# Four buffers instead of three and two for the weights between two feed-forward passes of an encoder kernel

## The chip, the cores and the metric

The kernel runs on one core of a Trainium2 chip. The metric is the device time of one execution in microseconds (us); the time before is 1585.03 us, the median of three runs (1584.3 to 1585.76).

## The reference

One encoder layer is applied to a prompt of 512 tokens and to a sample of 1024 tokens, both with 1024 channels, in float32:

```
x    = layer_norm(x)
h    = x @ w_in                               -> conv value | conv gate | rnn x | rnn gate
c    = silu(layer_norm(depthwise_conv31(value * sigmoid(gate))))
rec  = (rg_lru forward + rg_lru backward) * gelu(rnn gate)
x    = layer_norm(ALPHA * x + concat(c, rec) @ w_out)
u    = depthwise_conv3(x @ w_up)              -> val | gate, 2816 channels each
x    = layer_norm(ALPHA * x + (gelu(gate) * val) @ w_down)
```

## The kernel before, in words

The tokens are worked on in blocks of 512: the prompt (blk None), the second half of the sample (blk 1) and its first half (blk 0). Every product is made three times over, from a high and a low part of each operand (hi*hi, hi*lo, lo*hi); a weight therefore lies in SBUF as a pair, hi and lo.

**How a weight is made ready.** `weight` (L480) loads the raw tile (512 KB) into one of three staging buffers ST0 to ST2, and ScalarE (ACT) copies it, rounded, into the hi half of a weight slot. At the first use of a tile VectorE (DVE) or GpSimd (POOL) subtracts to get the lo half, which is then also stored to DRAM (`lo_out_d`, `lo_up_d`, `lo_down_d`); at a later use the lo half comes from there by a second DMA. A weight slot is a name such as W0; a `rot` list hands the names out in turn, and a new tile may enter a slot only when TensorE (PE) has read the old one for the last time.

**The stretch that the change touches** comes twice. In the first hand-over PE goes from the feed-forward pass of the prompt to that of blk 1, in the second from blk 1 to blk 0:

1. `up` tiles of `ffn` (L892): 44 tiles of 24 matmuls, weights in W0, W1, G3 by turns; their results go through three PSUM banks U0 to U2. `down` groups between them use A2, A3.
2. `residual` (L767): the output projection. For each half nh of the 1024 columns four weights kp, each used by 24 matmuls (four token tiles i, six each); slots by the list `WS` (L1014): W0, W1, G3 by turns.
3. `last` (L999): the last group of the down projection (pairs 18 to 21), held back so that PE has work while the layer norm `ln1` of the projection's result runs on DVE, ACT and POOL. It needs four weights of two chunks each: the first two serve nh = 0, the other two nh = 1, 48 matmuls per nh, in groups of twelve (token tile i). Slots: A2, A3 by turns. Between the groups PE transposes the four normalised token tiles (8 matmuls of 128x128 each, L269) for the next pass.
4. The `up` tiles of the next pass, whose input are these transposed tiles (B0 to B3).

**Other users of the slots.** G1 holds, at other times, the input `g` of the sample's token mixer `mixer_s` (L829), and behind it the layer-norm weights `gb` of the finished pass (`gb2a` L1024, `gb2b` L1036), which `ln2` multiplies and adds. A4 is the hi part of the projection's input for its first 512 channels (`split_block` L879, read by kp 0 and 1), then a buffer of `mixer_s` (L831) or of `ffn(0, ...)` (`a5`, L911). `mixer_s(0, ...)` runs beside the up tiles of blk 1: convolutions and scans on DVE, ACT and POOL, and small matmuls on PE (the recurrence gates) that stand between the up tiles.

**What sets the order.** `Sched.emit` (L273) places all operations before the program runs: it walks through a model of the engines and takes, on each, the ready operation of the best priority. What comes out is a fixed order on each engine and on the DMA queue of SP; at run time each engine follows its own order and waits by semaphores. So another slot name changes when an operation counts as ready, and with it the order. All DMAs are issued by SP (L250), one after the other: an issue that waits holds up those behind it.

```
w = weight(ws(), [("out", 4 * nh + kp, ALLC)], prio - 2, lo_eng="any", st=st)      # L767 residual
ws = rot(["W0", "W1", "G3"])                                                        # L898 ffn, up tiles
wdslot = rot(["A2", "A3"])                                                          # L901 ffn, down tiles
```

Of the kernel before, what the change touches and what calls it, by code (L numbers as in the profile page):

```python
# [12 lines left out]
ALU = mybir.AluOpType  # L13
# [5 lines left out]
NPAIR = DFF // 128  # L19
# [353 lines left out]
def body(ctx, tc, xp, xs, w_in, gw, w_out, w_up, w_down, par, gb, out_p, out_s):  # L373
# [3 lines left out]
    S = Sched(tc, sb, ps)  # L377
# [81 lines left out]
    def rot(names):  # L459
        st = {"i": 0}  # L460

        def nxt():
            st["i"] += 1
            return names[(st["i"] - 1) % len(names)]
        return nxt

    def split(hi, lo, src, prio, hi_eng="act", lo_eng="dve"):
        S.copy(hi_eng, hi, src, prio)
        S.tt(lo_eng, lo, src, hi.f32, ALU.subtract, prio)
# [83 lines left out]
    def mtile(w, xq, out, prio, parts=2, cols=slice(0, 512)):  # L553
        for q in range(parts):
            pairs = []
            for k in range(8 // parts * q, 8 // parts * (q + 1)):
                xh, xl = xk(xq, k, cols)
                c = slice(k * 128, (k + 1) * 128)
                pairs += prod3(w[0, c], w[1, c], xh, xl)
            S.mm(out, pairs, q == 0, q == parts - 1, prio)  # L560
# [328 lines left out]
    def tapcol(k):  # L889
        return P[C_FW:C_FW + 6 * NPAIR]._with(lambda a: a.rearrange("p (c k) -> p c k", k=3)[:, :, k])  # L890

    def ffn(blk, x1, y, PR, ev, wprio):  # L892

        va = S.buf("G0", [2, 2, 512])
        fb = [S.buf(n, [2, 2, 512], f32r) for n in (("A0", "A1", "GB") if blk == 0 else ("A0", "A1"))]
        ws = rot(["W0", "W1", "G3"])  # L898
        ub = rot([S.buf(f"U{i}", [512], psum=True) for i in range(3)])
        st = {"db": rot([S.buf(n, [512], psum=True) for n in ("U3", "M2")])}  # L900
        wdslot = rot(["A2", "A3"])  # L901
        first = blk is None
        lo = 1 if blk == 1 else 0
        if blk == 1:
            for b in fb:
                for i in range(2):
                    for h in range(2):
                        z = b[i, h, 0:1]
                        S.op("pool", 100, lambda z=z: nc.gpsimd.memset(z.f32(), 0.0), [], [z], ev)
        if blk == 0:  # L910
            a5 = S.buf("A4", [1024])  # L911
            ex = S.buf("ex", [2, 2])
            S.tt("dve", ut.all, sv[:, 0], tapcol(1), ALU.mult, ev)
            S.tt("dve", ut.all, ut.all, P[C_FB:C_FB + 2 * NPAIR], ALU.add, ev)
            t2 = S.buf("A5", [2 * NPAIR])
            S.tt("dve", t2.all, sv[:, 1], tapcol(2), ALU.mult, ev)
            S.tt("dve", ut.all, ut.all, t2.all, ALU.add, ev)
        def up(p):
            pr = PR + p * 0.01
            for s in range(2):  # L920
                m = s * NPAIR + p
                w = weight(ws(), [("up", m, ALLC)], wprio, lo_eng="any")
                u = ub()
                mtile(w, x1, u.all, pr)
                c = lambda k: col(C_FW + 3 * m + k)
                v = va[p % 2, s]
                acc = lambda a, b: va[p % 2, s, a:b]
                S.act(v, u.all, AF.Identity, c(1), col(C_FB + m), ev)
                S.stt(acc(1, 512), u[0:511], c(0), acc(1, 512), ALU.mult, ALU.add, ev)
                S.stt(acc(0, 511), u[1:512], c(2), acc(0, 511), ALU.mult, ALU.add, ev)  # L930
                if blk == 1:
                    S.copy("dve", sv[m], u[0:2], ev)
                if blk == 0:
                    S.stt(acc(511, 512), sv[m, 0:1], c(2), acc(511, 512), ALU.mult, ALU.add, ev)
                    S.stt(ex[p % 2, s:s + 1], u[511:512], c(0), ut[m:m + 1], ALU.mult, ALU.add, ev)
            S.act(va[p % 2, 1], va[p % 2, 1], AF.Gelu_apprx_tanh, prio=ev)
            if blk == 0:
                S.act(ex[p % 2, 1:2], ex[p % 2, 1:2], AF.Gelu_apprx_tanh, prio=ev)
                S.tt("dve", f5[p:p + 1], ex[p % 2, 0:1], ex[p % 2, 1:2], ALU.mult, ev)
            r = slice(lo, 512)  # L940
            S.tt("pool" if blk is None else "any", va[p % 2, 0, r], va[p % 2, 0, r], va[p % 2, 1, r], ALU.mult, ev)
            f = fb[(p // 2) % len(fb)]
            split(f[p % 2, 0, r], f[p % 2, 1, r], va[p % 2, 0, r], ev, lo_eng="dve")

        def wds(grp):

            chunks = [(nh, p) for nh in range(2) for p in grp]
            wd = {}

            def get(nh, p):  # L950
                if (nh, p) not in wd:
                    c = chunks.index((nh, p)) // 2 * 2
                    cs = chunks[c:c + 2]
                    w = weight(wdslot(), [("down", p_, slice(n_ * 512, (n_ + 1) * 512)) for n_, p_ in cs], wprio + 1,
                               lo_eng="any")
                    for i, ch_ in enumerate(cs):
                        wd[ch_] = (w, i)
                        if blk == 0:
                            n_, p_ = ch_
                            raw = raw_of[id(w)].buf[i * 512:(i + 1) * 512]  # L960
                            o = a5[n_ * 512:(n_ + 1) * 512]
                            if p_ == 0:
                                S.ts("dve", o, raw, f5[p_:p_ + 1], ALU.mult, prio=wprio)
                            else:
                                S.stt(o, raw, f5[p_:p_ + 1], o, ALU.mult, ALU.add, wprio)
                return wd[nh, p]
            return get

        def products(get, nh, i, ps_):
            pairs = []  # L970
            for p in ps_:
                w, ci = get(nh, p)
                wh, wl = w[0, ci * 512:(ci + 1) * 512], w[1, ci * 512:(ci + 1) * 512]
                f = fb[(p // 2) % len(fb)]
                fh, fl = f[p % 2, 0, i * 128:(i + 1) * 128], f[p % 2, 1, i * 128:(i + 1) * 128]
                pairs += [(fh, wh), (fh, wl), (fl, wh)]
            return pairs

        def down(gi, grp, banks=None, pr=None):
            get = wds(grp)  # L980
            pr = pr or PR + (grp[-1] + 0.5) * 0.01
            for nh in range(2):
                for i in range(4):
                    b = banks() if banks else st["db"]()
                    S.mm(b.all, products(get, nh, i, grp), True, True, pr)
                    yv = y[i // 2][i % 2, nh * 512:(nh + 1) * 512]
                    if gi == 0:
                        S.stt(yv, yv, ALPHA, b.all, ALU.mult, ALU.add, ev)
                    else:
                        S.tt("dve", yv, yv, b.all, ALU.add, ev)  # L990

        late = len(GROUPS) - (2 if blk == 0 else 1)
        for gi, grp in enumerate(GROUPS):
            for p in grp:
                up(p)
            if gi < late:
                down(gi, grp)

        def last():  # L999
            nonlocal wdslot  # L1000
            grp = GROUPS[-1]
            if blk != 0:
                banks = rot([S.buf(n, [512], psum=True) for n in ("M2", "C1")])
                down(len(GROUPS) - 1, grp, banks)
                return


            down(late, GROUPS[late], None, PR + 0.2105)
            wdslot = rot(["G2", "A5", "GW", "A6"])
            return wds(grp), grp, products  # L1010
        return last


    WS = ["W0", "W1", "G3"]  # L1014
    xcf1 = mixer_s(1, ("T2", "T3"), 32, 31)
    last_p = ffn(None, x1P, yP, 50.0, 6, 4)
    xc1 = split_block(xcf1, 33)
# [1 line left out]
    UB = ["U3", "M2", "C0", "C1", "U0", "U1", "U2", "U3"]  # L1019
    residual(1, 1, xc1, y1, 40, UB, rot(WS), pe=50.2105)  # L1020
    last_p()
# [9 lines left out]
    y0 = [S.buf("T0", [2, D]), S.buf("T1", [2, D])]  # L1031
    residual(1, 0, xc0, y0, 56, UB, rot(WS), pe=60.2105)
    last_1()
# [89 lines left out]
```

## Time and profile before

| | |
|---|---|
| median of three runs | 1585.03 us |
| the profiled execution | 1589.8 us |
| its span, first to last instruction | 1588.0 us |
| PE busy | 1551.1 us (98%) |
| DVE busy | 1183.7 us (75%) |
| ACT busy | 811.0 us (51%) |
| POOL busy | 159.9 us (10%) |
| mean granted clock of PE | 0.994 |
| DMA | 316.09 MB, 60.1% of 16 engines |

The profiled execution is one run; the span lies inside its time. Busy time of PE includes matmuls that wait in its pipeline, so it is read together with the idle time that the waits list, and with the granted clock.

### The profile page before, as it was taken

How to read it: one execution, taken by the hardware profiler on the slowest of the kernel's cores; microseconds unless marked ns; L12 is line 12 of the kernel's file. 1: busy time of each engine (PE TensorE's matmuls, PEld its weight loads, DVE VectorE, ACT ScalarE, POOL GpSimd, SP SyncE). 2: the span in 40 equal slices, each digit the busy share in tenths (PEclk: the TensorE clock that was granted, in tenths of full speed). 3: DMA queues.
4: the chain of work that ended last, by engine and by line, in shares of the span. 5: the costliest groups of instructions: out<-in, count | busy, mean ns of one | idle time of the engine just before them, and what ended most of it. 6: DMA issues, size and time to landing. Idle time of an engine off the chain costs nothing.

```text
span 1588.0 us, 19059 instructions
## 1 busy us (share of the span) xinstructions
PE 1551.1 (98%) x7012; PEld 1282.0 (81%) x7012; DVE 1183.7 (75%) x1841; ACT 811.0 (51%) x1013; POOL 159.9 (10%) x187
## 2 busy tenths in 40 slices
PE   6999999999999999999999999999999999999997
PEld 5888888888888888887788888888887888888885
DVE  8999995499999999953789899944338644545367
ACT  3637875149697873353359743352423433334351
POOL 3101111001212121010101100000001000000002
PEclk9999999999999999999999999999999999999998
DMA  9863335467566466756585776665675566665641
GB/s 373 304 215 108 118 120 187 159 197 246 152 220 205 156 207 234 213 164 240 178 277 194 228 249 208 197 228 195 196 223 190 187 198 203 197 196 184 199 148 67
DMA packets 107661, 316.09 MB, mean 199 GB/s; under 512 B 11952, under 2 KB 12080, under 8 KB 107440
## 3 DMA queue, kind: packets, MB, share of 16 engines
q1 hardware_dynamic: 107568, 314.88, 60.1%
q8 instruction: 55, 0.90, 0.2%
q14 instruction: 38, 0.31, 0.1%
HBM read 247.72 MB, written 67.11 MB: 198 GB/s over the span
## 4 chain that ended last, share of the span: by engine, by line
PE 78%; DVE 10%; ACT 6%; DMA 2%; issue 2%; POOL 0%; SPq 0%; DVEq 0%; POOLq 0%; ACTq 0%
PE b L261 76%; DVE b L209 5%; DVE b L200 4%; ACT b L239 4%; ACT L239 2%; PE b L269 2%; DMA b<-w_up 1%; DMA b<-lo_out_d 1%; DVE b L717 0%; DMA b<-xp 0%; DMA b<-lo_down_d 0%; POOL b L200 0%; DVE b L422 0%; SPq L250 0%; DVE b L424 0%
## 5 line engine op out<-in xcount | busy, mean ns | idle before, releaser
L261 PE MATMUL b<-b,b 128*128 128x512 f32 (+1 forms) x6724 | 1525.6, 388 | 8.7 <-DMA b<-lo_out_d 3.3
L261 PEld LDWEIGHTS b<-b,b 128*128 128x128 f32 x6724 | 1249.1, 189 | 270.4 <-DVE b L200 7.0
L209 DVE SCALAR_TENSOR_TENSOR b<-b,b,b 128x511 f32<-128x511 f32 (+11 forms) x850 | 588.7, 706 | 166.7 <-ACT b L239 143.5
L239 ACT ACTIVATE b<-b 128x1024 fp32r<-128x1024 f32 (+4 forms) x576 | 445.6, 799 | 471.7 <-PE b L261 219.8
L200 DVE TENSOR_TENSOR b<-b,b 128x512 f32<-128x512 f32 (+5 forms) x487 | 393.0, 826 | 121.0 <-ACT b L239 68.4
L239 ACT ACTIVATE b<-b,b 128x512 f32<-128x512 f32 (+1 forms) x337 | 257.5, 785 | 272.3 <-PE b L261 210.7
L200 POOL TENSOR_TENSOR b<-b,b 128x1 f32<-128x1 f32 (+2 forms) x85 | 88.2, 1043 | 1064.7 <-DVE b L223 542.9
L239 ACT ACT_TABLE_LOAD x100 | 128.3, 1283 | 23.2 <-DVE b L209 21.0
L209 DVE SCALAR_TENSOR_TENSOR b<-b,b 128x512 f32<-128x512 f32 (+2 forms) x81 | 50.2, 633 | 67.0 <-PE b L261 66.4
L200 POOL TENSOR_TENSOR b<-b 128x512 f32<-128x512 f32 x47 | 60.8, 1295 | 337.8 <-ACT b L239 154.7
L422 DVE BATCH_NORM_STATS2 b<-b 128x6 f32<-128x512 f32 x84 | 56.9, 689 | 17.7 <-PE b L269 11.9
L200 DVE TENSOR_TENSOR b<-b 128x512 f32<-128x512 f32 (+3 forms) x85 | 43.5, 528 | 21.5 <-ACT b L239 20.7
L269 PE MATMUL b<-b,b 128*128 128x128 f32 x288 | 40.2, 282 | 16.4 <-DVE b L209 15.5
L269 PEld LDWEIGHTS b<-b,b 128*128 128x128 f32 x288 | 34.3, 145 | 23.4 <-DVE b L209 11.0
L209 DVE SCALAR_TENSOR_TENSOR b<-b 128x512 f32<-128x512 f32 (+1 forms) x73 | 49.7, 691 | 3.8 <-ACT b L239 2.8
L717 DVE TENSOR_TENSOR_SCAN b<-b 128x512 f32<-128x512 f32 x24 | 29.4, 1223 | 0.7
L223 DVE TENSOR_SCALAR b<-b 128x1 f32<-128x1 f32 (+1 forms) x61 | 9.9, 166 | 1.7
L223 POOL TENSOR_SCALAR b<-b 128x1 f32<-128x1 f32 x37 | 9.9, 267 | 12.2 <-DVE b L200 8.7
L424 DVE BATCH_NORM_AGGREGATE b<-b 128x2 f32<-128x12 f32 (+1 forms) x48 | 9.6, 199 | 1.0
L246 DVE COPY b<-b 128x2 f32<-128x2 f32 x44 | 6.6, 151 | 0.0
L1044 POOL MEMSET b<- 128x128 f32 x1 | 0.2, 205 | 7.6 <-PE b L269 7.6
L223 DVE TENSOR_SCALAR b<-b,b 128x512 f32<-128x512 f32 x2 | 0.9, 484 | 0.0
(12 smaller groups left out, 1.9 us busy)
## 6 DMA issues: line engine op xcount, KB each, us to landing
b<-w_up SPq DMA_DIRECT2D x132, 512.0 KB, 4.5
b<-lo_up_d SPq DMA_DIRECT2D x88, 512.0 KB, 3.7
b<-w_down SPq DMA_DIRECT2D x132, 256.0 KB, 4.2
lo_up_d<-b SPq DMA_DIRECT2D x44, 512.0 KB, 5.3
b<-lo_down_d SPq DMA_DIRECT2D x88, 256.0 KB, 3.3
b<-w_in SPq DMA_DIRECT2D x32, 512.0 KB, 5.1
b<-w_out SPq DMA_DIRECT2D x24, 512.0 KB, 4.4
lo_down_d<-b SPq DMA_DIRECT2D x44, 256.0 KB, 5.2
```

What stands on the lines that cost most here:

```text
L200: return self.op(eng, cost if eng == "any" else cost[eng], lambda e=eng: self.engine(e).tensor_tensor(out=out(), in0=a(), in1=b(), op=op), ...
L209: o = self.op("dve", cost, lambda: self.nc.vector.scalar_tensor_tensor(out=out(), in0=a(), scalar=s() if isinstance(s, View) else s, in1=b ...
L223: return self.op(eng, cost, lambda: e.tensor_scalar(out=out(), in0=a(), scalar1=f(s1), scalar2=f(s2), op0=op0, **({"op1": op1} if op1 is n ...
L239: self.nc.scalar.activation(out=out(), in_=a(), func=func, **k)
L246: return self.op("dve", cost, lambda: self.nc.vector.tensor_copy(out(), a()), [a], [out], prio)
L261: self.nc.tensor.matmul(out=out(), lhsT=a(), rhs=b(), start=start and i == 0, stop=stop and i == len(pairs) - 1)
L269: self.nc.tensor.transpose(o(), i(), ident())
L422: S.op("dve", c.n * 1.0417 + 69, lambda i=i, c=c: nc.vector.bn_stats(out=sm_[6 * i:6 * i + 6](), in_=c()), [c], [sm_[6 * i:6 * i + 6]], prio)
L424: S.op("dve", 211, lambda: nc.vector.bn_aggr(out=sm_[12:14](), in_=sm_[0:6 * n]().rearrange("p (a b) -> p a b", a=n)), [sm_[0:6 * n]], [sm ...
L717: S.op("dve", out.n * 2.0833 + 69, lambda: nc.vector.tensor_tensor_scan(out=out(), data0=a(), data1=b(), initial=0.0, op0=ALU.mult, op1=AL ...
L1044: S.op("pool", 200, lambda: nc.gpsimd.memset(E0.all.f32(), 0.0), [], [E0.all], 60)
```

## The change

Three places. `WS`, the list of weight slots of the two output projections of the sample, has four names and starts with G1. `last` sets a four-name list for the held-back down group of the prompt and of blk 1. And for the last pair of the prompt's pass the multiplication of value and gate, which stood on POOL, may be put on DVE or POOL by the scheduler.

```diff
@@ ffn, up
-            S.tt("pool" if blk is None else "any", va[p % 2, 0, r], va[p % 2, 0, r], va[p % 2, 1, r], ALU.mult, ev)
+            S.tt("pool" if blk is None and p < NPAIR - 1 else "any", va[p % 2, 0, r], va[p % 2, 0, r], va[p % 2, 1, r], ALU.mult, ev)
@@ ffn, last
             if blk != 0:
+                wdslot = rot(["A2", "A3", "G1", "A4"])
                 banks = rot([S.buf(n, [512], psum=True) for n in ("M2", "C1")])
@@ body
-    WS = ["W0", "W1", "G3"]
+    WS = ["G1", "G3", "W0", "W1"]
```

No operation is added or taken away; the order on the engines moves. In the rows below bN is the N-th buffer that the program makes; N is the same buffer in both programs, the number behind it is not.

The first place is the DMA queue of SP ahead of the first hand-over. b467, b469, b471 and b473 are the first four weights of the output projection (kp 0 to 3), `lo_out_d` their lo halves, b513 the layer-norm weights `gb2a`, b496 those of `ln1`, b460 the residual input x0. Before:

```order
L250 DMA b513_5292<-gb 128x1024 x2
L250 DMA b454_5326<-w_up 128x1024
...
L250 DMA b470_5482<-w_out 128x1024
L250 DMA b471_5490<-lo_out_d_68 128x1024
L250 DMA b467_5540<-lo_out_d_68 128x1024
L250 DMA b496_5556<-gb 128x1024 x2
L250 DMA b472_5583<-w_out 128x1024
L250 DMA b460_5585<-x0s_d_64 128x1024 x2
L250 DMA b469_5595<-lo_out_d_68 128x1024
```

With the change:

```order
L250 DMA b467_5292<-lo_out_d_68 128x1024
L250 DMA b454_5325<-w_up 128x1024
...
L250 DMA b470_5484<-w_out 128x1024
L250 DMA b469_5492<-lo_out_d_68 128x1024
L250 DMA b471_5542<-lo_out_d_68 128x1024
L250 DMA b496_5558<-gb 128x1024 x2
L250 DMA b478_5585<-w_out 128x1024
L250 DMA b460_5587<-x0s_d_64 128x1024 x2
L250 DMA b473_5597<-lo_out_d_68 128x1024
```

The lo halves of the first three projection weights now stand ahead of b496, and only that of the fourth (b473) where that of the second (b469) stood. b513 is gone from here; it now stands 43 rows further on, behind the first lo halves of the next pass:

```order
L250 DMA b563_6005<-lo_down_d_70 128x512 x2
L250 DMA b577_6009<-lo_down_d_70 128x512 x2
L250 DMA b568_6014<-w_up 128x1024
L250 DMA b513_6119<-gb 128x1024 x2
L250 DMA b567_6175<-lo_up_d_69 128x1024
L250 DMA b572_6182<-w_up 128x1024
```

There it waits until PE has read the third weight of the held-back group (b493, now in G1) for the last time.

The second place is PE in the second half (nh = 1) of the held-back group of the second hand-over. b719 and b721 are its third and fourth weight, b712 and b713 the PSUM banks, b687 the third and fourth normalised token tile, which the transposes (L269) read. Before:

```order
L269 MATMUL b734_9067<-b2_100,b687_7121 128x128 x4
L269 MATMUL b735_9073<-b2_100,b687_7121 128x128 x4
L261 MATMUL b712_8948<-b719_9059,b552_6126 128x512 x6
L261 MATMUL b712_8948<-b721_9063,b551_6116 128x512 x6
L261 MATMUL b713_8991<-b719_9059,b552_6126 128x512 x6
L261 MATMUL b713_8991<-b721_9063,b551_6116 128x512 x6
L269 MATMUL b737_9133<-b2_100,b687_7121 128x128 x4
L269 MATMUL b738_9139<-b2_100,b687_7121 128x128 x4
```

With the change:

```order
L261 MATMUL b712_8958<-b719_8861,b552_6128 128x512 x6
L261 MATMUL b712_8958<-b721_8891,b551_6123 128x512 x6
L269 MATMUL b734_9095<-b2_100,b687_7038 128x128 x4
L269 MATMUL b735_9103<-b2_100,b687_7038 128x128 x4
L261 MATMUL b713_9004<-b719_8861,b552_6128 128x512 x6
L261 MATMUL b713_9004<-b721_8891,b551_6123 128x512 x6
L261 MATMUL b712_8958<-b719_8861,b552_6128 128x512 x6
L261 MATMUL b712_8958<-b721_8891,b551_6123 128x512 x6
```

Both pairs of transposes stand one group of twelve matmuls later than before. In the first hand-over only the earlier pair does (the later pair keeps its place).

The third place is DVE around the first hand-over. b489, b491, b493, b495 are the four weights of the held-back group (the rows make their lo halves), b474 is the first PSUM bank of the projection's second half, whose sum opens `ln1`. Before, b493 and b495 stand in the middle of `ln1`; with the change they stand ahead of it:

```order
L200 TENSOR_TENSOR b491_5748<-b490_5702,b491_5748 128x1024
L200 TENSOR_TENSOR b493_5794<-b492_5751,b493_5794 128x1024
L200 TENSOR_TENSOR b495_5821<-b494_5721,b495_5821 128x1024
L209 SCALAR_TENSOR_TENSOR b460_5587<-b460_5587,b474_5736 128x512
L422 BN_STATS b501_5719<-b460_5587 128x6
```

Besides these, POOL takes over two of the eight multiplications and additions of `ln2` in the first hand-over (none before), and two instead of one in the second, and the one of the prompt's last pair goes from POOL to DVE.

## Rows read from the trace of the kernel before

**Rows 1.** The page: busy time of the engines, and granted clock in 40 slices.
```profile
PE 1551.1 (98%) x7012; PEld 1282.0 (81%) x7012; DVE 1183.7 (75%) x1841; ACT 811.0 (51%) x1013; POOL 159.9 (10%) x187
...
PEclk9999999999999999999999999999999999999998
```

**Rows 2.** Waits of PE over the whole span: total us, times, longest us.
```profile
PE b L261 <- DMA b<-lo_out_d: 3.3, 1, 3.3
PE b L261 <- DVE b L200: 2.5, 5, 0.9
PE b L261 <- DMA b<-lo_down_d: 2.0, 1, 2.0
```

**Rows 3.** Timeline of PE, 711 to 742: start, length, instructions, [idle before, releaser].
```profile
711.18 11.38 PE L261 MATMUL b<-b,b 128*128 128x512 f32 x49
725.82 16.54 PE L261 MATMUL b<-b,b 128*128 128x512 f32 x59 [3.26 <-DMA b<-lo_out_d]
```

**Rows 4.** Stretches: length, busy us (count) by engine, granted clock, DMA share, GB/s.
```profile
726.00:732.00 6.00, 6.00 (x15) 4.65 (x16) 0.00 (x0) 0.00 (x0) 0.00 (x0) 0.50 0.48 191
...
1203.00:1206.50 3.50, 3.39 (x8) 2.21 (x9) 2.95 (x4) 1.21 (x2) 0.00 (x0) 0.51 0.58 223
```

**Rows 5.** Timeline of PE, 1186 to 1216.
```profile
1188.36 5.73 PE L261 MATMUL b<-b,b 128*128 128x512 f32 x24
...
1198.05 1.06 PE L269 MATMUL b<-b,b 128*128 128x128 f32 x8 [0.35 <-DVE b L209]
...
1202.90 6.03 PE L261 MATMUL b<-b,b 128*128 128x512 f32 x17 [2.00 <-DMA b<-lo_down_d]
...
1209.56 6.64 PE L261 MATMUL b<-b,b 128*128 128x512 f32 x28
```

**Rows 6.** Timeline of PE, 764 to 796.
```profile
781.88 8.26 PE L261 MATMUL b<-b,b 128*128 128x512 f32 x35 [0.94 <-DVE b L200]
790.71 1.06 PE L269 MATMUL b<-b,b 128*128 128x128 f32 x8 [0.57 <-DVE b L424]
791.53 4.81 PE L261 MATMUL b<-b,b 128*128 128x512 f32 x20
```

**Rows 7.** DMA issues at 717.5, 703.8, 711.5 and 677.5: KB each, median us to landing.
```profile
b<-lo_out_d SPq DMA_DIRECT2D x1, 512.0 KB, 8.3
...
b<-lo_out_d SPq DMA_DIRECT2D x1, 512.0 KB, 3.6
...
b<-gb SPq DMA_DIRECT2D x2, 512.0 KB, 6.8
...
b<-gb SPq DMA_DIRECT2D x2, 512.0 KB, 4.6
```

**Rows 8.** Stretches, as rows 4: the held-back group's halves, then the mixer.
```profile
766.60:779.60 13.00, 12.94 (x66) 10.52 (x64) 12.66 (x20) 5.44 (x7) 1.37 (x3) 1.00 0.28 81
779.60:794.40 14.80, 13.25 (x65) 10.73 (x66) 14.66 (x26) 7.37 (x9) 2.19 (x5) 1.00 0.55 181
...
800.00:1040.00 240.00, 240.00 (x1066) 198.06 (x1065) 216.56 (x349) 138.31 (x168) 19.22 (x20) 1.00 0.69 227
```

**Rows 9.** Timelines of DVE, POOL and SP, 793 to 830 and 1220 to 1225.
```profile
793.91 2.94 DVE L200 TENSOR_TENSOR b<-b,b 128x1024 f32<-128x1024 f32 x3
...
800.91 1.52 DVE L209 SCALAR_TENSOR_TENSOR b<-b,b,b 128x511 f32<-128x511 f32 x2
...
811.73 1.78 SPq L250 DMA_DIRECT2D b<-mixs_d  x2
...
829.13 1.29 POOL L200 TENSOR_TENSOR b<-b,b 128x512 fp32r<-128x512 f32 x1 [22.34 <-ACT b L239]
...
1220.86 1.23 DVE L200 TENSOR_TENSOR b<-b,b 128x1024 f32<-128x1024 f32 x1
...
1222.22 2.40 POOL L200 TENSOR_TENSOR b<-b,b 128x1024 f32<-128x1024 f32 x1 [2.97 <-ACT b L239]
...
1223.57 1.06 DVE L209 SCALAR_TENSOR_TENSOR b<-b,b,b 128x1 f32<-128x1 f32 x1
```

## The prediction

> **What bounds the kernel now.** I read the page first. PE is busy for 1551.1 of 1588.0 us, DVE for 75%, and PE's granted clock is at its upper level in nearly every slice [rows 1]. So the time is PE's work plus what PE loses, and a change of buffers, which adds and removes no matmul, can be worth only what PE loses in the stretches that it touches. The waits of PE come second [rows 2]: one for a lo half of the output projection (3.3 us), one for a lo half of the down projection (2.0 us) and five for what DVE subtracts or multiplies (2.5 us in all). The timelines of PE place them: 3.26 us ahead of 725.82 is the second weight of the projection (kp 1) in the first hand-over [rows 3]; 2.00 us ahead of 1202.90 is the fourth weight of the held-back down group in the second hand-over [rows 5]; 0.94 us ahead of 781.88 is that group's third weight in the first hand-over [rows 6]. These are the places where the slots turn too early.
>
> A wait costs PE more than its length. After each of the two long ones the granted clock is 0.50 and 0.51, that is 1.2 instead of 2.4 GHz [rows 4], and the matmuls behind it run slowly. At full clock a matmul takes 0.228 us: 28 in 6.64 against 24 in 5.73 us [rows 5]. Behind the first wait 59 take 16.54 us where 49 at full clock take 11.38 [rows 3]: 16.54 - 11.38 - 10 x 0.228 = 2.88 us lost. Behind the second 17 take 6.03 us, where 6.64 - 11 x 0.228 = 4.13 would do [rows 5]: 1.90 us lost. After the 0.94 us the 35 matmuls that follow take 8.26 us, that is full speed [rows 6].
>
> **The change, part by part.**
>
> *Four slots for the projection.* Before, kp 1 takes W1 and must wait until the last up tile has been read; its lo half is issued at 717.5, behind the two loads of `ln1`'s weights and beside x0, and lands 8.3 us later, where one issued at 703.8 took 3.6 us [rows 7]. Now kp 0 goes to G1, free long before, and kp 1 to G3, whose lo half is issued where that of kp 2 was, at 703.8. kp 2 (W0) is issued ahead of the crowd too. Only kp 3 (W1) stands in the crowd: if it lands where kp 1's lo half does now, at 725.8, it is still early: kp 0's matmuls end where the wait begins, at 722.6 [rows 3], so PE reaches kp 3 after two weights more of 24 x 0.228 = 5.47 us, at 722.6 + 10.9 = 733.5. The wait and its slow matmuls go: 3.26 + 2.88 = **6.1 us**.
>
> *Four slots for the held-back group, first hand-over.* The third and fourth weight (b493, b495) no longer wait for A2 and A3, so the 0.94 us goes. Their lo halves, 1.23 us each on DVE [rows 9], move from the middle of `ln1` to ahead of it. That matters for the next wait: the last transposes wait 0.57 us for `ln1` [rows 6], and DVE is full there, 12.66 of 13.00 and 14.66 of 14.80 us [rows 8]. With 2.5 us less on DVE `ln1` ends about 2.5 us earlier, while PE arrives only 0.94 us earlier; 0.57 - 2.5 + 0.94 is below nothing, so this wait goes as well. Gain 0.94 + 0.57 = **1.5 us**.
>
> *The same in the second hand-over.* Here the lo halves come by DMA, and b719 and b721 can be loaded when the projection leaves G1 and A4: that is at least two weights (10.9 us) before the group begins, and its first half (13.0 us [rows 8]) passes before PE needs them, 24 us in all against landings of 3.6 to 8.3 us [rows 7]. The wait of 2.00 and the 1.90 us behind it go. The 0.35 us ahead of the transposes at 1198.05 [rows 5] goes too, since these now stand behind twelve matmuls (2.7 us). What is late next is `ln1`'s last tile: PE comes to the last transposes about 4.2 us earlier but 2.7 us later by their new place. The two hand-overs use the same DVE chain, so I take 0 for a new wait and let up to 1 us stand in the range. Gain 2.00 + 1.90 + 0.35 = **4.2 us**.
>
> *What it costs.* G1 now holds a weight until almost the end of the held-back group, so `gb2a` and `gb2b` are loaded after it, not 100 us ahead. The last read of G1 is six matmuls before the hand-over is done, 1.4 us; the two loads land 4.6 us later when alone and 6.8 us in a crowd [rows 7], that is 3.2 to 5.4 us after the hand-over. Before, `ln2`'s first multiplication by them ran at 793.91, half a us ahead of it [rows 9] (the hand-over is done at 791.53 + 12 x 0.228 = 794.3 [rows 6]). In DVE's queue two multiplications of 1.23 us now stand ahead of the first eviction of the next pass, which ran at 800.91, 6.6 us after the hand-over [rows 9]. With loads that land at 3.2 us nothing is late; at 5.4 the eviction starts 5.4 + 2.5 - 6.6 = 1.3 us late. The cover is the three banks U0 to U2: PE needs the first again only three tiles after its start, 16 us after the hand-over. If that cover were gone, PE would wait those 1.3 us.
>
> `ln2` also ends the old use of G1, and the mixer's first load into it follows, at 811.73 before [rows 9], 17.4 us after the hand-over. From it hang ACT, DVE and POOL work and the first recurrence gate on PE. The order puts that gate 156 matmuls behind the hand-over instead of 168 (counted in PE's order), so 2.7 us earlier. Before it stood at about 794.3 + 168 x 0.228 = 832.6, and its last input came from POOL at 829.13 + 1.29 = 830.4 [rows 9]: 2.2 us to spare. So the gate is due 0.5 us before its input if the mixer starts as late as before. The change takes two of `ln2`'s eight steps off DVE, which may bring the start forward. Bounds: nothing, or 0.5 us, plus 2.2 us if the loads land as in a crowd, plus 2.4 us if one POOL step more stands ahead. I take **0.4 us**, nearest to the row of before, since the modelled order had the mixer beside 240 us of PE with no wait at all [rows 8].
>
> *The rest.* The multiplication of the prompt's last pair goes from POOL to DVE; its result is read only by the held-back group, behind the whole projection of 8 x 5.47 = 44 us, so it costs nothing. The loads of the first up tiles come earlier or at the same place, and W0, W1 and G3 end in the same last use, so the next pass starts from the same slots.
>
> POOL's two steps of 2.40 us meet a full DVE: one DVE instruction on a single element took 1.06 us beside such a step [rows 9]. I count that inside the 2.4 us above. The Trainium skill (SBUF — State Buffer, Who interferes with whom) says that a VectorE instruction with two SBUF inputs and a GpSimd instruction that reads SBUF exclude each other, and that the loser waits for the whole of the other. By that rule 2 x 2.40 = 4.8 us of DVE are lost in the first hand-over, and if all of it reached PE the sum would be 11.9 - 4.8 = 7.1 us (an estimate), near the first rival's.
>
> **Sum.** 6.1 + 1.5 + 4.2 - 0.4 = 11.5 us with the digits kept (6.14 + 1.51 + 4.25 = 11.9 before the cost). Against the profiled execution's 1589.8 us that is 1578.3; the median of the runs is 1585.03, 4.8 us lower, and the difference taken off it gives **1573.5 us**.
>
> **The rivals.**
>
> *A new wait in the mixer's gates takes back a part.* For it: DVE is busy 216.56 of 240 us there [rows 8], the margin of the first gate turns negative, and the first load waits for `ln2`, which now waits for a DMA. Against it: lateness of a chain that DVE sets is paid once, not at each gate, and PE itself has come earlier by the whole gain. Price: 0.5 + 2.2 = 2.7 us of idle, and with slow matmuls in the ratio of the first wait, (3.26 + 2.88) / 3.26 = 1.88, 5.1 us. Time 1585.0 - 11.9 + 5.1 = 1578.2 us.
>
> *The first wait stays.* SP issues in order, and kp 3's lo half stands behind the loads of `ln1`'s weights, a raw tile and x0. If it took twice the 8.3 us, PE would stop at kp 3 instead of kp 1, and the change would not do there what it says. Then 1585.0 - 11.5 + 6.1 = 1579.6 us. Against it: 733.5 - 725.8 = 7.7 us to spare.
>
> *The waits are shorter without the profiler.* The profiled execution is 4.8 us longer than the median. If all of that lay in these DMA waits, only 11.5 - 4.8 = 6.7 us would come back: 1578.3 us. Nothing in the rows says where the 4.8 us lie.
>
> *Slower: `gb2a` stops DVE.* Its first use stands in DVE's queue ahead of the evictions; if it lands late, evictions, gates and the banks U0 to U2 all stop behind it. Once three banks are full every us is PE's, times up to 1.88. The change turns into a loss when this costs more than 11.9 us, that is at some 6.3 us of idle: a landing some 17 us after the issue, over twice the slowest row for it (6.8). At 8 us of idle: 1585.0 - 11.9 + 15.0 = 1588.1 us.
>
> **How the numbers follow.** Forecast 0.62, the gates 0.20, the first wait 0.06, the profiler 0.07, `gb2a` 0.05. The range reaches from 1571.5 (no new wait, and another us from the lesser waits of the hand-overs) to 1579.3, which takes in the profiler's case, the middle of the gates' case and most of that of the first wait; about 0.15 is left out. A measurement of this kernel can tell 0.2%, 3.2 us, from no change. Faster by more: 0.62 + 0.16 + 0.03 + 0.07 = 0.88. Within it: 0.04 of the gates and 0.03 of the first wait, 0.07. Slower: 0.05.
>
> **What would show it.** In the changed kernel PE's waits for `lo_out_d` and `lo_down_d` are gone, the granted clock stays at 1.00 in both hand-overs, and no wait over 0.3 us stands between the projection's start and the next up tiles. The loads of `gb` come right at the hand-overs and `ln2`'s first multiplication 3 to 5 us behind them. The prediction is wrong if PE shows waits above 1 us for gates or evictions in the 50 us behind a hand-over, or if kp 3 waits for its lo half.

## The result, and the profile after

| | before | after |
|---|---|---|
| median, measured beside each other (four runs each) | 1585.39 us (1584.3 to 1585.76) | 1575.66 us (1575.55 to 1575.73) |
| ratio, with 95% interval | | 0.994 (0.9926 to 0.9953) |
| the profiled execution | 1589.8 us | 1575.68 us |
| its span | 1588.0 us | 1573.9 us |
| PE, DVE, POOL busy | 1551.1, 1183.7, 159.9 us | 1544.7, 1180.5, 167.6 us |

The kernel is 9.7 us faster; 11.5 were forecast. The profiled executions differ by more, 14.1 us. Why these are two numbers is the main lesson of this case.

The page of the changed kernel, for [rows 1]:

```profile
PE 1544.7 (98%) x7012; PEld 1280.6 (81%) x7012; DVE 1180.5 (75%) x1839; ACT 809.1 (51%) x1012; POOL 167.6 (11%) x189
...
PEclk9999999999999999999999999999999999999998
```

PE has the same 7012 instructions and is busy for 6.4 us less; the 2.88 and 1.90 us by which the matmuls behind the two long waits were slow [rows 3, 5] are most of it. All waits of PE, for [rows 2] (us in total, times, longest):

```profile
PE b L269 <- DVE b L209: 15.0, 2, 10.9
PE b L261 <- DVE b L200: 1.7, 4, 0.6
PE b L261 <- POOL b L200: 0.3, 1, 0.3
```

No wait for a DMA is left. The first line belongs to the start of the program, the others to places outside the two hand-overs. The timelines of PE at the first hand-over's projection, its held-back group, and the second hand-over, for [rows 3, 6, 5]:

```profile
710.91 24.32 PE L261 MATMUL b<-b,b 128*128 128x512 f32 x106
...
775.42 1.03 PE L269 MATMUL b<-b,b 128*128 128x128 f32 x8
776.22 5.71 PE L261 MATMUL b<-b,b 128*128 128x512 f32 x24
781.76 1.04 PE L269 MATMUL b<-b,b 128*128 128x128 f32 x8
782.55 13.66 PE L261 MATMUL b<-b,b 128*128 128x512 f32 x59
...
1191.85 5.73 PE L261 MATMUL b<-b,b 128*128 128x512 f32 x24
1197.42 1.03 PE L269 MATMUL b<-b,b 128*128 128x128 f32 x8
1198.21 18.18 PE L261 MATMUL b<-b,b 128*128 128x512 f32 x79
```

No row has a bracket: PE runs through both hand-overs without a wait, and 106 matmuls take 24.32 us, 0.229 us each, where 59 took 16.54. The stretches, for [rows 4] and the second of [rows 8] (length, busy us by engine, granted clock, DMA share, GB/s):

```profile
726.00:732.00 6.00, 6.00 (x28) 4.99 (x27) 0.00 (x0) 1.06 (x1) 0.00 (x0) 1.00 0.88 321
1200.00:1203.50 3.50, 3.50 (x17) 2.91 (x16) 3.19 (x9) 2.38 (x2) 1.63 (x4) 1.00 0.76 223
770.80:785.60 14.80, 14.80 (x74) 12.38 (x74) 14.41 (x26) 5.49 (x7) 2.17 (x5) 1.00 0.33 113
```

The clock is 1.00 in all three; 28 matmuls start in the 6 us that had 15. Two groups of DMA issues, the lo half of kp 3 (issued at 717.23) and `gb2a` (issued at 784.21), for [rows 7] (KB each, median us to landing):

```profile
b<-lo_out_d SPq DMA_DIRECT2D x1, 512.0 KB, 7.2
...
b<-gb SPq DMA_DIRECT2D x2, 512.0 KB, 4.5
```

Last, POOL and DVE behind the first hand-over, which ends at 785.40, for [rows 9]:

```profile
788.88 2.36 DVE L200 TENSOR_TENSOR b<-b,b 128x1024 f32<-128x1024 f32 x2
793.35 1.53 DVE L209 SCALAR_TENSOR_TENSOR b<-b,b,b 128x511 f32<-128x511 f32 x2 [2.11 <-ACT b L239]
...
798.39 1.53 DVE L209 SCALAR_TENSOR_TENSOR b<-b,b,b 128x511 f32<-128x511 f32 x2
```

```profile
798.61 2.41 POOL L200 TENSOR_TENSOR b<-b,b 128x1024 f32<-128x1024 f32 x1 [4.88 <-ACT b L239]
...
816.97 1.31 POOL L200 TENSOR_TENSOR b<-b,b 128x512 fp32r<-128x512 f32 x1 [1.59 <-ACT b L239]
```

`ln2`'s first multiplication stands 3.5 us behind the hand-over, the first eviction 8.0 us behind it (6.6 before), and the input of the first recurrence gate is there at 816.97 + 1.31 = 818.28.

**One sum to compare all profiles.** At full speed a 128x512 matmul starts 0.227 us after the one ahead of it (0.114 us where a matmul has 256 columns or, in a transpose, 128). What the distances from start to start in the trace exceed this, summed, is what PE lost in a stretch: waits and low clock together. Over the whole span that is 27.5 us in the profile of before and 13.5 in that of after, and the profiled time less this sum is 1589.8 - 27.5 = 1562.3 and 1575.7 - 13.5 = 1562.2 us. It comes to 1561.8 to 1562.4 us in all thirteen profiles of this study. So the time of this kernel is a constant and PE's lost time, and the places of the loss can be laid side by side (us; the columns are 712 to 740, 740 to 880 and 1180 to 1212 us of the trace; below nothing means no loss, the nominal distances being rounded):

| profile | projection, first | held-back group and gates, first | second hand-over | whole span | profiled time |
|---|---|---|---|---|---|
| before, first profile | 6.4 | 2.6 | 4.8 | 27.5 | 1589.8 |
| before, second | 4.4 | 3.5 | 3.0 | 23.9 | 1586.2 |
| before, third | 4.4 | 3.0 | 3.1 | 23.5 | 1585.6 |
| before, fourth | 4.9 | 3.0 | 2.9 | 25.5 | 1587.7 |
| after | 0.0 | 0.1 | 0.0 | 13.5 | 1575.7 |
| after, second profile | 0.0 | 0.0 | -0.1 | 13.2 | 1575.1 |
| projection's list alone | 0.0 | 3.0 | 2.9 | 18.9 | 1581.2 |
| held-back list alone | 4.6 | 0.0 | 0.1 | 17.3 | 1579.5 |
| four names, old start | 1.9 | 1.5 | -0.1 | 16.0 | 1578.4 |
| three names, new start | 0.0 | 1.2 | 0.0 | 14.9 | 1577.1 |
| POOL keeps the multiplication | 0.0 | 0.0 | 0.0 | 13.7 | 1575.8 |
| first hand-over alone | 0.0 | -0.1 | 3.1 | 16.0 | 1578.2 |
| held-back list of three | 0.0 | 1.9 | 4.4 | 19.3 | 1581.1 |

### The profile page after: what moved, and what is told of

Read it like the earlier page. It is cut to its first block, busy times and chain, and to the rows that moved or that the text cites. A ratio compares the mean times of both kernels' runs of the same rounds, so it can differ in the third digit from the quotient of the medians.

```text
span 1573.9 us, 19061 instructions
## 1 busy us (share of the span) xinstructions
PE 1544.7 (98%) x7012; PEld 1280.6 (81%) x7012; DVE 1180.5 (75%) x1839; ACT 809.1 (51%) x1012; POOL 167.6 (11%) x189
## 4 chain that ended last, share of the span: by engine, by line
PE 84%; DVE 7%; ACT 5%; issue 2%; DMA 1%; POOL 0%; DVEq 0%; SPq 0%; POOLq 0%; ACTq 0%
PE b L261 82%; DVE b L209 4%; ACT b L239 3%; DVE b L200 3%; PE b L269 2%; ACT L239 2%; DMA b<-xp 0%; DMA b<-w_up 0%; DVE b L717 0%; POOL b L200 0%; DVE b L422 0%; SPq L250 0%; DVEq L1120 0%; POOLq L1120 0%; POOL b L223 0%
## 5 line engine op out<-in xcount | busy, mean ns | idle before, releaser
L209 DVE SCALAR_TENSOR_TENSOR b<-b,b,b 128x511 f32<-128x511 f32 (+12 forms) x850 | 587.4, 705 | 171.2 <-ACT b L239 149.7
L200 POOL TENSOR_TENSOR b<-b,b 128x1 f32<-128x1 f32 (+3 forms) x87 | 94.0, 1084 | 1059.3 <-DVE b L223 553.6
L200 POOL TENSOR_TENSOR b<-b 128x512 f32<-128x512 f32 (+1 forms) x47 | 60.7, 1293 | 323.9 <-ACT b L239 157.9
L269 PE MATMUL b<-b,b 128*128 128x128 f32 x288 | 40.3, 282 | 15.2 <-DVE b L209 15.0
L269 PEld LDWEIGHTS b<-b,b 128*128 128x128 f32 x288 | 34.5, 145 | 21.7 <-DVE b L209 10.9
L223 POOL TENSOR_SCALAR b<-b 128x1 f32<-128x1 f32 x37 | 12.1, 326 | 11.2 <-DVE b L200 8.3
```

The costliest lines, as they stand in the source:

```text
L200: return self.op(eng, cost if eng == "any" else cost[eng], lambda e=eng: self.engine(e).tensor_tensor(out=out(), in0=a(), in1=b(), op=op), ...
L209: o = self.op("dve", cost, lambda: self.nc.vector.scalar_tensor_tensor(out=out(), in0=a(), scalar=s() if isinstance(s, View) else s, in1=b ...
L223: return self.op(eng, cost, lambda: e.tensor_scalar(out=out(), in0=a(), scalar1=f(s1), scalar2=f(s2), op0=op0, **({"op1": op1} if op1 is n ...
L269: self.nc.tensor.transpose(o(), i(), ident())
```

## The experiments

The theory was that of the prediction: three places where a slot turns too early, each worth its wait and the slow matmuls behind it. The rival that needed a test first was that the profiled execution of before showed longer waits than the others do.

### The kernel before, three more profiles

No edit. For the second profile:

> The kernel before, unchanged, for a second profile. Theory A: the two DMA waits of the hand-overs (3.26 and 2.00 us) are the same in every execution, so the new profile shows them again within 0.3 us, and about 1589.8 us. Theory B: their lengths change from execution to execution, and the first profile caught long ones; the new profile then shows a time nearer to the median of 1585.4 us, with some 4 us less of waits and of matmuls at the low clock in the two hand-overs, and the other stretches alike. Theory C: profiling itself adds the 4.8 us; then the waits are the same and the time is lost elsewhere.

Measured: 1586.22 us. PE's waits for a DMA in it:

```profile
PE b L261 <- DMA b<-lo_out_d: 2.5, 1, 2.5
PE b L261 <- DMA b<-lo_down_d: 2.1, 1, 2.1
```

The first wait is 0.8 us shorter than in [rows 2], the second as long. But behind the second the clock did not fall. Its timeline and the stretch behind it:

```profile
1201.16 4.14 PE L261 MATMUL b<-b,b 128*128 128x512 f32 x17 [2.06 <-DMA b<-lo_down_d]
```

```profile
1201.20:1205.10 3.90, 3.90 (x17) 3.17 (x18) 3.14 (x4) 1.64 (x2) 0.00 (x0) 1.00 0.52 185
```

The same 17 matmuls that took 6.03 us behind a wait of 2.00 us [rows 5], at a granted clock of 0.51 [rows 4], here take 4.14 us at 1.00. The two hand-overs lose 7.4 us, in the first profile 11.2: this 3.9 us is the 3.6 us by which the execution is shorter. Theory B holds, with an addition: not only the waits differ from execution to execution, but also whether the clock falls behind one. Theory C falls: a profiled execution at 1585 to 1586 us is among the others.

The third and the fourth profile were to show whether the hand-overs are all that varies:

> The kernel before, a third profile. Theory: what its executions differ by lies in the two hand-overs alone, in how long PE waits for lo_out_d and lo_down_d and whether the clock falls behind the wait; the matmul time above 0.227 us each that the profile shows at 720 to 735 and 1195 to 1210 us (11.3 us in the first profile, 7.3 in the second) and the profiled execution's time move together, one us for one us: time = 1578.5 us + that sum, within 1 us. Rival: something else in the execution varies, and the time differs by some us at the same sum.

> The kernel before, a fourth profile, for the same question: time = 1578.5 us + the sum lost in the two hand-overs, within 1 us, against a time that differs at the same sum.

Measured: 1585.61 us with 7.5 us lost in the hand-overs, which makes 1578.1, and 1587.71 us with 7.8, which makes 1579.9 and is 0.4 us outside the bound. The fourth execution has two small waits more for DVE, at 669.10 (0.26 us) and 926.29 us (0.31 us), and loses 0.6 us more at the start of the program. So the hand-overs carry most of the variation, not all; with PE's loss over the whole span the times agree within 0.3 us (table).

The stretch from 712 to 740 us in the first four profiles of before, in their order, shows the same by a count; the number behind PE's busy time is that of matmuls started in 28 us (125 in the kernel after). First profile:

```profile
712.00:740.00 28.00, 24.74 (x97) 19.82 (x96) 5.99 (x7) 11.54 (x14) 1.29 (x1) 0.88 0.70 241
```

Second, third, fourth:

```profile
712.00:740.00 28.00, 25.53 (x106) 20.62 (x105) 6.93 (x10) 11.60 (x13) 1.29 (x1) 0.94 0.71 253
```

```profile
712.00:740.00 28.00, 25.51 (x105) 20.58 (x104) 6.95 (x9) 11.43 (x13) 1.29 (x1) 0.94 0.72 253
```

```profile
712.00:740.00 28.00, 25.04 (x104) 20.13 (x103) 6.47 (x9) 12.64 (x15) 1.29 (x1) 0.94 0.69 247
```

The first profile misses 28 matmuls, the others 19 to 21. The wait varies with the landing of one DMA, the lo half of kp 1: it took 8.3 us in the first profile [rows 7], 7.5, 7.5 and 8.0 in the others, and PE waited 3.26, 2.47, 2.49 and 2.96 us. The price behind the wait varies too, and by more: the first column less the wait is 3.2 us in the first profile and 1.9 in each of the others.

### Each list alone

```diff
-    WS = ["W0", "W1", "G3"]
+    WS = ["G1", "G3", "W0", "W1"]
```

> Only the four names of the projection's list; the held-back group keeps its two, and the prompt's last pair its multiplication on POOL. Main theory: the wait for lo_out_d and the slow matmuls behind it go, the waits of the held-back group stay. With the sizes of the prediction 1585.4 - 6.1 = 1579.3 us. Rival, most of the gain comes from the held-back group: 1583 us or more. In the trace the wait for lo_down_d (about 2.0 us) stays in the second hand-over, and lo_out_d is not among PE's waits.

Measured: 1581.80 us (1580.84 to 1582.81), ratio 0.9977 (0.9968 to 0.9986), before 1585.22 us beside it. The gain is 3.4 us, not 6.1, though the wait is gone: the first column of the table has 0.0. The time lies between the main theory's 1579.3 and the rival's 1583 us. The held-back group's waits stayed, as expected:

```profile
PE b L261 <- DMA b<-lo_down_d: 1.7, 2, 1.0
PE b L269 <- DVE b L424: 0.6, 1, 0.6
```

The other list alone:

```diff
             if blk != 0:
+                wdslot = rot(["A2", "A3", "G1", "A4"])
```

> Only the four names of the held-back group. Main theory: the first wait (lo_out_d, 3.3 us, low clock behind it) stays, those of the held-back group go in both hand-overs: 1585.4 - 1.5 - 4.2 = 1579.7 us. If the parts simply add up, the gains of this run and of the run with the projection's list alone sum to the 9.7 us of the whole change. Rival: with G1 and A4 taken by the group but the projection's slots as before, the mixer's start comes later and part is lost, 1582 us or more, with waits of PE for DVE or POOL behind the first hand-over.

Measured: 1579.43 us (1578.24 to 1580.37), ratio 0.9963 (0.9951 to 0.9976). The gain is 5.8 us, the forecast was 5.7. The first wait stays and is the only one for a DMA:

```profile
PE b L261 <- DMA b<-lo_out_d: 2.7, 1, 2.7
```

The parts add up: 3.4 + 5.8 = 9.2 of 9.7 us. The rival falls, since behind the first hand-over no wait came (0.0 in the second column). The larger part of the gain is the held-back group's, as the rival of the run before had it, but not by as much as that rival's 1583 us would need.

### The first hand-over alone

The second projection keeps three names that start with W0, and the four names of the held-back group hold only for the prompt:

```diff
+                if blk is None:
+                    wdslot = rot(["A2", "A3", "G1", "A4"])
...
-    residual(1, 0, xc0, y0, 56, UB, rot(WS), pe=60.2105)
+    residual(1, 0, xc0, y0, 56, UB, rot(["W0", "W1", "G3"]), pe=60.2105)
```

> The change in the first hand-over alone: the second projection has three names with W0 first, the second held-back group A2 and A3. Theory: the first hand-over shows no wait for lo_out_d and none over 0.3 us, the second still waits for lo_down_d by 1 to 2 us; of the excess that the profiles show there (4.8 us in the first profile of before, 2.9 in the second, 3.0 with the projection's list alone) 3 to 4.8 us stay: 1578.7 to 1580.5 us. Rival: the second hand-over costs nothing outside the profiled executions: 1576.5 us or less.

Measured: 1578.56 us (1577.68 to 1578.98). Against 1575.66 us the second hand-over is worth 2.9 us, the lower end of what was expected (0.1 us under it), where the prediction had 4.2; the rival, 1576.5 us or less, falls. Its profile loses 3.1 us there, and the granted clock stays at 1.00 behind the waits, which are shorter ones:

```profile
PE b L261 <- DMA b<-lo_down_d: 1.7, 3, 1.1
```

### Which slot comes first, and how many there are

The whole change with another projection list, once with four names and the old start, once with three and the new start:

```diff
-    WS = ["G1", "G3", "W0", "W1"]
+    WS = ["W0", "W1", "G3", "G1"]
```

> The whole change, but the projection's list is W0, W1, G3, G1: four names with the old start. Theory: what matters is that kp 1 does not stand in W1, which the last up tiles still hold; here it does, so its lo half is issued in the crowd as before, and the first wait stays: 1575.7 + 6.1 = 1581.8 us with a wait for lo_out_d of 3 us and granted clock at 0.50 behind it. Rival: the number of slots matters and not which comes first; then 1575.7 us and no such wait.

```diff
-    WS = ["G1", "G3", "W0", "W1"]
+    WS = ["G1", "G3", "W0"]
```

> The whole change, but the projection's list has three names and the new start: G1, G3, W0. Theory: what keeps kp 1 out of W1 is the start of the list, not its length. kp 3 then enters G1 when kp 0 has been read (about 722.6 in the first profile of before), and its lo half, 3.6 to 8.3 us behind its issue, is there by 731, before PE reaches kp 3 at 733.5. So 1575.7 us as with four names, within 0.3 us, and no wait for lo_out_d. Rival: the fourth slot is needed too; then PE waits for a lo half of the projection by 1 to 3 us, with the low clock behind it where the wait is over 2 us: 1577 to 1580 us, and a spread of some us between the runs, as every kernel so far has that shows such a wait.

Measured: 1580.76 us (1578.44 to 1583.95) and 1577.35 us (1576.44 to 1577.67). With the old start the wait is there, in this execution a short one. Timeline of PE, and the stretch behind it:

```profile
723.11 17.07 PE L261 MATMUL b<-b,b 128*128 128x512 f32 x74 [1.67 <-DMA b<-lo_out_d]
```

```profile
723.10:727.00 3.90, 3.89 (x17) 3.24 (x18) 0.00 (x0) 1.06 (x1) 0.00 (x0) 1.00 1.01 390
```

The clock stays at 1.00 and little beyond the 1.67 us is lost. This profile is of the quickest of ten executions; they spread over 5.5 us. The first theory holds: which slot comes first is what matters. The 5.1 us at the median are not all due to it, though: this kernel also loses 1.5 us behind its held-back group (second column), since its last transposes stand elsewhere in the order, as they do in the kernel with three names below. That leaves 3.4 us against the kernel with three names and some 3.7 us against the change.

With three names and the new start PE has no wait for the projection, as the theory said, but the time is 1.7 us above the change, as the rival said. The cause is neither's. The timeline of PE at the end of its first hand-over:

```profile
784.49 1.04 PE L269 MATMUL b<-b,b 128*128 128x128 f32 x8
786.04 0.50 PE L261 MATMUL b<-b,b 128*128 128x512 f32 x1 [0.51 <-ACT b L239]
786.77 13.45 PE L261 MATMUL b<-b,b 128*128 128x512 f32 x58 [0.22 <-DVE b L200]
```

With three names the placed order puts the last transposes behind all of the held-back group, and the next pass waits for their copies (0.51 us for the hi part, 0.22 us for the lo part; 1.2 us in the table). With the change twelve matmuls, 2.7 us, lie behind them. So the fourth name is worth something here by the order that it happens to give, not by its slot.

### POOL keeps the last pair's multiplication

```diff
-            S.tt("pool" if blk is None and p < NPAIR - 1 else "any", va[p % 2, 0, r], va[p % 2, 0, r], va[p % 2, 1, r], ALU.mult, ev)
+            S.tt("pool" if blk is None else "any", va[p % 2, 0, r], va[p % 2, 0, r], va[p % 2, 1, r], ALU.mult, ev)
```

> The whole change, but the prompt's last pair has its multiplication on POOL again. Theory: it is read only by the held-back group, 44 us later, so nothing changes: 1575.7 us within 0.2 us. Rival: POOL's longer step makes a lo half or DVE late: a new wait of PE of 0.3 us or more between 640 and 720 us, and a time 0.3 to 2 us longer.

Measured: 1575.72 us (1575.32 to 1575.91). The difference of 0.06 us lies within the spread: this part of the change does nothing that can be measured, and the rival's new wait of PE did not come.

### Three names for the held-back group

```diff
-                wdslot = rot(["A2", "A3", "G1", "A4"])
+                wdslot = rot(["A2", "A3", "A4"])
```

> The whole change, but the held-back group has three names, A2, A3, A4, so that G1 is free for gb2a and gb2b ahead of the hand-over, and the group's fourth weight must wait for A2. Theory: one slot more is not enough; the fourth weight's lo half comes as late as before, so the second hand-over waits for lo_down_d again (about 2 us) and the first for DVE (about 0.5 to 0.9 us): 1578 to 1580 us. Rival: the loads that compete are halved by the slot that is free, so the fourth lands in time, and the gb loads ahead of the hand-over give back the 0.4 us that was put down as the change's cost: 1575.3 to 1576 us.

Measured: 1580.67 us (1579.86 to 1582.57). By the number the first theory is right, within 0.7 us; by the mechanism it is not. The lo half of the fourth weight landed at 1192.02, when PE wanted it at 1192.04 us, and no wait for lo_down_d is left: on this point the rival was right. In the first hand-over the theory holds, with a wait of 0.65 us for DVE. PE's list of waits, its timeline in the second hand-over and the stretch behind the wait:

```profile
PE b L269 <- DVE b L200: 2.1, 1, 2.1
```

```profile
1190.57 5.73 PE L261 MATMUL b<-b,b 128*128 128x512 f32 x24
1198.43 1.15 PE L269 MATMUL b<-b,b 128*128 128x128 f32 x8 [2.13 <-DVE b L200]
```

```profile
1199.00:1202.00 3.00, 3.00 (x12) 2.44 (x11) 2.17 (x5) 1.12 (x2) 0.85 (x3) 0.55 0.55 175
```

The last transposes stand where they stood before, right behind 24 matmuls, and now PE arrives there 2.13 us ahead of `ln1`'s last tile; the clock falls to 0.55 behind it. The DMA wait became a wait for DVE of the same size. In the whole change the transposes stand twelve matmuls later, and there `ln1` is done at 1197.19 and PE comes at 1197.42 us: 0.23 us to spare. So in the second hand-over the order matters as well as the slots.

### The changed kernel again

> The changed kernel again. Theory: since it has no wait of PE for a DMA, its executions hardly differ: 1575.7 us, all within 0.5 us of each other, while those of the kernel before spread over 6 to 7 us on the same chip. Rival: the four runs shown so far were alike by chance, and some execution lies 2 us or more above the others.

Measured: 1575.03 us (1574.48 to 1575.9), ratio 0.9928 (0.9909 to 0.9948), with a second profile that has no wait for a DMA. Its runs are 1.4 us apart, more than the 0.5 expected; the seven of before beside them are 5.1 us apart, and those of all the comparisons span 1582.07 to 1589.62 us. With the waits the change removed most of the variation too. No run beat the change beyond this spread.

## Why the prediction was right, and where it was off

The sign, the places and the time (1575.66, forecast 1573.5, range 1571.5 to 1579.3) are as predicted; the sizes are not. By medians the 9.7 us divide so: leaving out the projection's list costs 1579.43 - 1575.66 = 3.8 us, and adding it alone gains 3.4; leaving out both lists in the second hand-over costs 2.9; the rest, 3 us, goes to the held-back group in the first, which no run has by itself.

- **Four slots for the projection: 6.1 us forecast, 3.4 to 3.8 measured.** The mechanism is right: kp 3's lo half landed at 717.23 + 7.2 = 724.4, where 725.8 was forecast, some 9 us before PE wanted it. The size is off because 3.26 us of wait and 2.88 us of slow matmuls were read from one execution that had more of both than the next three (6.4 us lost there against 4.4 to 4.9). Why the medians give less than even these three profiles lose is not shown.
- **The second hand-over: 4.2 forecast, 2.9 measured.** The same: 4.8 us lost in the first profile, 2.9 to 3.1 in the other three. The 0 taken for `ln1` was right by 0.23 us, thanks to the later place of the transposes.
- **The held-back group in the first hand-over: 1.5, and 0.4 of cost behind it; some 3 us measured.** In the profiles of before this place loses 2.6 to 3.5 us, after it 0.1 at most. The waits were named rightly, but their size was read from the idle time in brackets. From start to start the same two waits of the first profile, with the short gap ahead of the first, cost 0.26 + 1.19 + 0.73 = 2.2 us, and the first gates around 845 us another 0.4, which went as well. What was missed besides is that the first gates did not become later: their input is there at 818.28, 2.5 us before the gate runs at 820.76, where -0.5 us was forecast. The mixer's first load comes 17.8 us behind the hand-over (17.4 before), so its start did not move forward; but the input to the first gate is there 32.9 us behind it (36.1 before). The gain lies behind the landing of that load: 8.3 us from there to the input, 12.1 before. All of `ln2` stands ahead of the load, so its two steps that left DVE are not the reason; no run shows which part of the new order is. The step that failed is the 0.4 us: it took the start of the mixer as the only thing that could move.
- **The subtraction.** The sum was made against the profiled execution and 4.8 us taken off both sides to come to the median. That holds only if the 4.8 us lie outside the waits that go. They lay mostly inside: three more profiles lose 7.4 to 7.8 us in the hand-overs' long waits against 11.2. So the third rival (0.07) described what happened, and its wording, that the profiler was the cause, was wrong: runs of before without a profile reach 1589.62 us too, and profiled ones 1585.61. Against its own execution the sum was too small, 11.5 for 14.1 us; against the median it was too large, 11.5 for 9.7. The two errors go opposite ways, 2.6 us too little in the terms and 4.4 us too much by the subtraction, so it is in part luck that the forecast came within 2.2 us of the time.
- **Rivals that fell.** The gates took back nothing. The first wait did not stay at kp 3. The two loads of `gb2a` landed 4.1 and 4.9 us after their issue, 2.9 and 4.1 us behind the hand-over, where 3.2 to 5.4 were forecast. The first eviction came 8.0 - 6.6 = 1.4 us later than before, near the bound of 1.3, though for another reason: DVE waited for ACT and ACT for POOL, not for the loads. Two small steps of `ln2` on POOL, 0.55 and 0.27 us long the time before, took 1.47 and 0.76 us while DVE ran its two multiplications (788.88 to 791.24), 1.41 us more together. Timelines of POOL and ACT:

```profile
787.41 0.55 POOL L200 TENSOR_TENSOR b<-b,b 128x1 f32<-128x1 f32 x1 [1.19 <-DVE b L223]
788.05 0.27 POOL L223 TENSOR_SCALAR b<-b 128x1 f32<-128x1 f32 x1
789.04 1.47 POOL L200 TENSOR_TENSOR b<-b,b 128x1 f32<-128x1 f32 x1 [0.71 <-DVE b L223]
790.61 0.76 POOL L223 TENSOR_SCALAR b<-b 128x1 f32<-128x1 f32 x1
```

```profile
791.40 1.91 ACT L239 ACTIVATE b<-b,b 128x1024 f32<-128x1024 f32 x2 [1.80 <-POOL b L223]
```

  The three banks covered it as argued: PE has no wait there.
- **POOL beside DVE.** The two evictions of 798.39 to 799.92 ran while POOL did its step of 2.41 us, and took 1.53 us, as two of this form do in the mean. The group in the list of the costliest, by form (busy us, mean ns):

```profile
L209 DVE SCALAR_TENSOR_TENSOR b<-b,b,b 128x511 f32<-128x511 f32 x296 | 221.4, 748 | 155.0 <-ACT b L239 148.9
```

  The Trainium skill (SBUF — State Buffer, Who interferes with whom) says that a VectorE instruction with at most one SBUF input, outside VectorE's two-port modes, does not contend with GpSimd; one of the two inputs of these lies in PSUM, and the trace agrees. The 4.8 us of the estimate were not paid, since the steps lay mostly beside such instructions and beside DVE's idle 2.11 us. A multiplication of DVE with both inputs in SBUF that began 0.34 us before the second step's end took 0.88 us, where its form takes 0.70 in the mean:

```profile
800.68 0.88 DVE L200 TENSOR_TENSOR b<-b 128x511 f32<-128x511 f32 x1 [0.69 <-ACT b L239]
```

  The larger price was paid the other way round, by the small steps of POOL in the point above.

## What to carry to other kernels

Before a gain is sized from one profile, its time is compared with the median: where it is longer, a wait for a DMA in a crowd is the first place for the difference, and a gain read from it can be too large by most of that (here the long waits held 3.5 to 3.9 of the 4.8 us). Idle time in brackets is not the whole of a wait either; the distance from start to start is. A slot that comes free early is worth more than a slot more; where the list starts decided some 3.5 us here. When a wait goes, look at what stands next on the same engine and how far it is ahead of its input: with 0.23 us to spare the gain held, and with the old order it turned into another wait of the same length.

## What the runs showed of the hardware that was not expected

- Waits of PE of nearly one length cost different amounts. Behind 2.00 us of idle the granted clock was 0.51 (half speed, 1.2 GHz), behind 2.06 us at the same place in another execution 1.00, behind 2.13 us 0.55. Behind 1.67 us it stayed at 1.00, behind 2.5 to 3.3 us it fell each time that it was seen (five profiles), with 1.9 to 3.2 us lost besides the wait. So the bound of 2 us that one expectation names is none.
- The same DMA of 512 KB, issued at the same place in the queue, landed after 7.5 to 8.3 us in four executions of one program, and each tenth of a us is in PE's wait.
- A step of POOL on 128x1 elements that took 0.55 us otherwise took 1.47 us beside two multiplications of DVE, in the same place in five profiles (after, its second profile, held-back list alone, first hand-over alone, POOL keeps the multiplication), and it delayed the first eviction by way of ACT. No run sets the two apart.
